# A row sum behind ReLU: the first load cut from 16 rows of each partition to one

## The chip, the core and the metric

The kernel runs on one core of a Trainium2 chip. The metric is the device time of one execution in microseconds (us). Three runs of the kernel before gave 161.19, 161.30 and 161.29 us; the median is 161.29.

The engines that matter here: ACT (ScalarE) and DVE (VectorE) compute, SP (SyncE) issues every DMA, and sixteen DMA engines move the data between HBM and the on-chip memory of 128 partitions.

## The reference

```python
def setup_inputs():
    batch, seq, dim = 32, 512, 1024
    return {"x": np.random.randn(batch, seq, dim).astype(np.float32)}

def reference(x):
    relu_x = np.maximum(x, 0)
    return np.sum(relu_x, axis=-1).astype(np.float32)
```

The input is 16,384 rows of 1,024 float32, 64 MiB; the output is one float32 for each row, 64 KiB.

## The kernel before, in words

**Tiling.** Each of the 128 partitions gets 128 rows. `x` is cut in two regions. The first holds 128 x 16 rows: partition p takes 16 rows that lie one behind the other, so the region is one stretch of 8 MB and the pitch from partition to partition is 64 KB. The second holds the other 14,336 rows, 112 for each partition, with a pitch of 448 KB. `rows(m, n)` and `sums(m, n)` (lines 85 and 90) choose the region for the rows m to m + n of each partition, for loads and stores.

**Stages.** Seven blocks of 16 rows (`ROWS`, 8,192 KB each) go through three buffers `io0` to `io2` of 64 KB for each partition. The eighth and last 16 rows are cut finer: a load of 8 rows, one of 4 (`TAIL = [8, 4]`), and then 4 rows as two loads of 1,164 and 642 KB and two small pieces (`piece0`, `piece1`, 120 and 122 KB). Row c + 2 of these four is put together from five parts: 280 elements of the first load, 260 of the second, the two pieces of 240 and 244, and a last reduction that also adds the other partial sums (line 224, 247 elements).

**Who computes.** In blocks 0 to 5 ACT clamps with ReLU in place (`clamp`, line 117) and DVE sums the clamped rows (`total`, line 125). `TWO` says in what steps: the whole block of 16 rows in blocks 0 to 2, twice 8 in blocks 3 and 4, twice 7 in block 5, where ACT does the two rows left by itself. A row alone is done in one instruction, either by ACT (`act_row`, line 132) or by DVE (`dve_row`, line 140). Block 6 is 9 rows of ACT and 7 of DVE. In the tail loads the rows alternate: row i goes to ACT if i is even, or if the load has 8 rows and i is 7, and otherwise to DVE.

**Order and waits.** The instructions of each engine run in the order of the program. `load` (line 99) issues on SP. The loads of blocks 0, 1 and 2 wait for nothing. The load of block j from 3 on waits until DVE is done with block j - 3 (`freed`), and the first tail load until DVE is done with block 4. Each load has a semaphore of its own, on which its first ACT row and, where DVE reads loaded rows, its first DVE row waits. A DVE sum waits for the ACT clamp before it. The stores stand behind all loads on SP: 16 sums of each partition (block 0), then 110, then the last 2 (`store`, line 110).

**Opening.** `open_without_barrier` puts the first `EARLY = 1` load ahead of everything else on SP and takes the opening barrier out.

Of the kernel before, what the change touches and what calls it, by code (L numbers as in the profile page):

```python
# [4 lines left out]
F32 = mybir.dt.float32  # L5
RELU = mybir.ActivationFunctionType.Relu
MAX, ADD = mybir.AluOpType.max, mybir.AluOpType.add
P = 128

ROWS = 16  # L10
# [3 lines left out]
TWO = [[16], [16], [16], [8, 8], [8, 8], [7, 7], []]  # L14
# [2 lines left out]

TAIL = [8, 4]  # L20
START_PIECE, END_PIECE = 280, 260
PIECES = [240, 244]

EARLY = 1


def kernel(tc: tile.TileContext, x: bass.AP, out: bass.AP):
    nc = tc.nc
    sems = Semaphores(tc)

    tc.close()
    tc.compile()
    nc.cur_bb = nc.bb_map[tc.start_bb_name]
    body = nc.cur_bb.bb.instructions
    ends = list(body)
    body.clear()
    n_stores = relu_sum(nc, sems, x, out)
    body.extend(ends)


    nc.cur_bb = nc.bb_map[tc.start_bb_name + "_end"]
    nc.cur_bb.bb.instructions.clear()
    nums = sorted(s.num for s in (*sems.loads, sems.act, sems.dve))
    cleared = range(nums[0], nums[-1] + 1)
    assert len(cleared) == len(nums)
    nc.sync.sem_clear(cleared)
    nc.sync.wait_ge(sems.stored, 16 * n_stores).then_inc(sems.stored, -16 * n_stores)
    open_without_barrier(tc, EARLY)


class Semaphores:
    def __init__(self, tc: tile.TileContext):
        n = len(TWO) + len(TAIL) + 2 + len(PIECES)
        self.loads = [tc.alloc_semaphore(f"load{i}") for i in range(n)]
        self.act = tc.alloc_semaphore("act")
        self.dve = tc.alloc_semaphore("dve")
        self.stored = tc.alloc_semaphore("stored")


def relu_sum(nc, sems: Semaphores, x: bass.AP, out: bass.AP):  # L60
    x_flat = x.flatten_outer_dims()
    N, D = x_flat.shape
    NT = N // P
    NB = len(TWO)
    assert N == P * NT == P * ROWS * (NB + 1)
    assert sum(TAIL) == ROWS - 4 and START_PIECE + END_PIECE + sum(PIECES) == D

    bufs = [nc.alloc_sbuf_tensor(f"io{i}", [P, ROWS, D], F32) for i in range(NBUF)]
    res = nc.alloc_sbuf_tensor("res", [P, NT], F32)

    extra = len(PIECES) + 1
# [3 lines left out]
    ]  # L75


    N1 = P * ROWS
    xf = x_flat[:N1].rearrange("(p m) d -> p m d", p=P)
    xv = x_flat[N1:].rearrange("(p m) d -> p m d", p=P)  # L80
    o_flat = out.rearrange("b s -> (b s)")
    of = o_flat[:N1].rearrange("(p m) -> p m", p=P)
    ov = o_flat[N1:].rearrange("(p m) -> p m", p=P)

    def rows(m, n):
        if m < ROWS:
            return xf[:, m : m + n, :]
        return xv[:, m - ROWS : m - ROWS + n, :]

    def sums(m, n):  # L90
        if m < ROWS:
            return of[:, m : m + n], res[:, m : m + n]
        return ov[:, m - ROWS : m - ROWS + n], res[:, m : m + n]

    n_load = n_act = n_dve = n_store = 0

    def load(dst, src, after=None):
        nonlocal n_load
        dma = nc.sync.dma_start(out=dst, in_=src)  # L99
        if after:  # L100
            dma.wait_op(sems.dve, after[1], "sem-ge")
        dma.then_inc(sems.loads[n_load], 16)
        n_load += 1
        return sems.loads[n_load - 1]

    def store(m, n, act, dve):
        nonlocal n_store
        dst, src = sums(m, n)
        nc.sync.wait_ge(sems.act, act)
        nc.sync.dma_start(out=dst, in_=src).wait_op(sems.dve, dve, "sem-ge").then_inc(  # L110
            sems.stored, 16
        )
        n_store += 1
# [24 lines left out]
    def dve_row(ap, accum_out, loaded):  # L138
        nonlocal n_dve
        i = nc.vector.tensor_scalar(  # L140
            out=ap,
            in0=ap,
            scalar1=0.0,
            scalar2=None,
            op0=MAX,
            op1=ADD,
            accum_out=accum_out,
        )
        if loaded is not None:
            i.wait_op(loaded, 16, "sem-ge")  # L150
        i.then_inc(sems.dve, 1)
        n_dve += 1

    freed = []
    m = 0
    for j in range(NB):
        buf = bufs[j % NBUF]
        loaded = load(buf[:, :, :], rows(m, ROWS), j >= NBUF and freed[j - NBUF])
        c = 0
        act_waits = dve_waits = loaded  # L160
        for n in TWO[j]:
            clamp(buf[:, c : c + n, :], act_waits)
            total(buf[:, c : c + n, :], m + c, n)
            act_waits = None
            c += n
        for _ in range(ACT[j]):
            act_row(buf[:, c, :], res[:, m + c : m + c + 1], act_waits)
            act_waits = None
            c += 1
        for _ in range(DVE[j]):  # L170
            dve_row(buf[:, c, :], res[:, m + c : m + c + 1], dve_waits)
            dve_waits = None
            c += 1
        assert c == ROWS
        freed.append((n_act, n_dve))
        m += ROWS
# [3 lines left out]
    c = 0  # L180
    for n in TAIL:
        loaded = load(
            buf[:, c : c + n, :], rows(m, n), None if c else freed[NB - NBUF]
        )
        for i in range(n):
            if i % 2 == 0 or (n == 8 and i == 7):
                act_row(buf[:, c, :], res[:, m : m + 1], loaded if i == 0 else None)
            else:
                dve_row(buf[:, c, :], res[:, m : m + 1], loaded if i == 1 else None)
            c += 1  # L190
            m += 1

    flat = buf[:, :, :].rearrange("p c d -> p (c d)")
    src = rows(m, 4).rearrange("p c d -> p (c d)")
    at = c * D
    split = 2 * D
# [4 lines left out]
    loaded = load(flat[:, at : at + b], src[:, :b])  # L201
    act_row(buf[:, c, :], res[:, m : m + 1], loaded)
    sums_act = n_act
    dve_row(buf[:, c + 1, :], res[:, m + 1 : m + 2], loaded)
    sums_dve = n_dve
    dve_row(flat[:, at + split : at + b], others[0], None)
    loaded = load(flat[:, at + end : at + 4 * D], src[:, end:])
# [7 lines left out]

    store(0, ROWS, *freed[0])
    store(ROWS, NT - ROWS - 2, sums_act, sums_dve)

    for i in range(len(PIECES) - 1):
        dve_row(parts[i][:, :], others[2 + i], arrived[i])
# [9 lines left out]
    ).wait_op(sems.dve, n_dve, "sem-ge").then_inc(sems.dve, 1)  # L232
    n_dve += 1
    store(NT - 2, 2, n_act, n_dve)
    return n_store


def open_without_barrier(tc: tile.TileContext, n_loads: int):

    SP = mybir.EngineType.SP
    blocks = tc.nc.main_func.blocks
    opening = blocks[0].instructions
    body = next(b for b in blocks if b.name == tc.start_bb_name).instructions
    for i in list(opening):
        if isinstance(i, (mybir.InstDrain, mybir.InstEventSemaphore)):
            opening.remove(i)
    loads = [i for i in body if i.engine == SP][:n_loads]
    for i in loads:  # L250
        assert isinstance(i, mybir.InstDMACopy)
        body.remove(i)
    at = next(n for n, i in enumerate(opening) if i.engine == SP)
    opening[at:at] = loads
# [30 lines left out]
```

## Time and profile before

One execution was profiled. Its span, from the first instruction to the last, is 159.6 us.

| | |
|---|---|
| median of three runs | 161.29 us |
| span of the profiled execution | 159.6 us |
| DVE busy | 117.6 us (74%) |
| ACT busy | 104.2 us (65%) |
| bytes moved | 67.18 MB, 421 GB/s over the span |
| DVE, sum of 16 rows | 17.22 us |
| DVE, sum of 8 rows | 8.68 us |
| ACT, clamp of 16 rows | 13.86 us |
| ACT, clamp of 8 rows | 7.02 us |
| ACT, one row with its sum | 1.05 us |
| DVE, one row with its sum | 1.21 us, a new one each 1.14 us |
| first load, issue to landing | 21.6 us |
| other blocks, issue to landing (median) | 26.9 us |

The shares of busy time are means over the whole span; the engines wait for different things in different parts of it, so single stretches have to be looked at. A DVE row is followed by a short read of the accumulator, and the next row starts while that is read. An arrow in square brackets behind a line of the timeline gives the engine's idle time before the instruction and what ended it.

### The profile page before, as it was taken

The page shows a single profiled execution, that of the slowest core. Times are in us where ns is not written, and L with a number is a line of the kernel's source. Part 1 is how long each engine was busy: PE and PEld are TensorE (multiplying, and loading weights), DVE is VectorE, ACT ScalarE, POOL GpSimd, SP SyncE. Part 2 cuts the span into 40 slices and gives each one's busy share as a digit, 9 for nine tenths or more (in the row PEclk, how much of TensorE's full clock was granted, in tenths as well). Part 3 has the DMA queues.
Part 4 walks back from the last instruction along what each step waited for, and adds up shares of the span by engine and source line. Part 5 has one row for each costly group of instructions (what it writes and reads, how often), then busy time and mean ns, then how long its engine had stood idle before and what let it go on. Part 6 is the DMA issues. An engine that isn't in the chain of part 4 may idle for free.

```text
span 159.6 us, 120 instructions
## 1 busy us (share of the span) xinstructions
DVE 117.6 (74%) x43; ACT 104.2 (65%) x50; POOL 0.2 (0%) x4
## 2 busy tenths in 40 slices
DVE  0000000009999499994999999999999999999986
ACT  3000059990699708996099951999329993499995
POOL 0000000000000000000000000000000000000000
DMA  7996996996997999979979969969969969798993
GB/s 279 509 526 263 526 526 263 526 509 279 526 476 312 526 394 394 526 345 443 526 328 460 526 263 526 526 263 526 509 279 526 493 296 526 337 452 382 418 412 119
DMA packets 2304, 67.18 MB, mean 421 GB/s; under 512 B 640, under 2 KB 896, under 8 KB 1024
## 3 DMA queue, kind: packets, MB, share of 16 engines
q1 hardware_dynamic: 2304, 67.18, 98.0%
HBM read 67.11 MB, written 0.07 MB: 421 GB/s over the span
## 4 chain that ended last, share of the span: by engine, by line
DMA 43%; DVE 34%; ACT 17%; another core or an unknown queue 3%; SPq 1%; issue 0%
DMA io<-in_x_dram 43%; DVE res L125 32%; ACT io L117 17%; DVE io L140 1%; SPq L99 1%; DVE piece L224 0%; DVE piece L140 0%
## 5 line engine op out<-in xcount | busy, mean ns | idle before, releaser
L125 DVE TENSOR_REDUCE res<-io 128x8 f32<-128x8192 f32 (+2 forms) x9 | 101.1, 11287 | 40.0 <-ACT io L117 40.0
L117 ACT ACTIVATE io<-io 128x8192 f32<-128x8192 f32 (+2 forms) x9 | 81.7, 9110 | 47.7 <-DMA io<-in_x_dram 47.7
L132 ACT ACTIVATE io<-io 128x1024 f32<-128x1024 f32 x20 | 20.9, 1045 | 6.0 <-DMA io<-in_x_dram 6.0
L140 DVE TENSOR_SCALAR_CACHE_REDUCE io<-io 128x1024 f32<-128x1024 f32 (+2 forms) x15 | 15.8, 1110 | 0.5 <-DMA io<-in_x_dram 0.4
L132 ACT ACTIVATION_READ_ACCUMULATOR io<-io 128x1 f32 x20 | 3.8, 188 | 0.0
L117 ACT ACT_TABLE_LOAD x1 | 1.3, 1283 | 0.1
L140 DVE DVE_READ_ACCUMULATOR io<-io 128x1 f32 x15 | 1.2, 82 | 0.0
L224 DVE TENSOR_SCALAR_CACHE_REDUCE piece<-piece 128x247 f32<-128x247 f32 x1 | 0.4, 410 | 0.0
L140 DVE TENSOR_SCALAR_CACHE_REDUCE piece<-piece 128x240 f32<-128x240 f32 x1 | 0.4, 397 | 0.0
L269 POOL MEMSET const-bfloat16-1.0<- 128x1 bf16 x1 | 0.1, 101 | 0.0
L269 POOL MEMSET const-uint8-127<- 128x1 uint8 x1 | 0.1, 101 | 0.0
L269 POOL MEMSET const-float32-0.0<- 128x1 f32 x1 | 0.1, 98 | 0.2 <-issue 0.2
L269 POOL MEMSET const-float32-1.0<- 128x1 f32 x1 | 0.1, 98 | 0.0
L224 DVE DVE_READ_ACCUMULATOR piece<-piece 128x1 f32 x1 | 0.1, 83 | 0.0
L140 DVE DVE_READ_ACCUMULATOR piece<-piece 128x1 f32 x1 | 0.1, 82 | 0.0
## 6 DMA issues: line engine op xcount, KB each, us to landing
io<-in_x_dram SPq DMA_DIRECT2D x1, 4096.0 KB, 21.6
io<-in_x_dram SPq DMA_DIRECT2D x1, 2048.0 KB, 26.1
io<-in_x_dram SPq DMA_DIRECT2D x1, 1164.0 KB, 28.4
io<-in_x_dram SPq DMA_DIRECT2D x1, 642.0 KB, 29.5
piece<-in_x_dram SPq DMA_DIRECT2D x1, 122.0 KB, 29.2
piece<-in_x_dram SPq DMA_DIRECT2D x1, 120.0 KB, 29.4
io<-in_x_dram SPq DMA_DIRECT2D x7, 26.9
out_dram<-res SPq DMA_DIRECT2D x1, 55.0 KB, 1.6
```

What stands on the lines that cost most here:

```text
L99: dma = nc.sync.dma_start(out=dst, in_=src)
L117: i = nc.scalar.activation(out=ap, in_=ap, func=RELU)
L125: nc.vector.tensor_reduce(out=res[:, m : m + n], in_=ap, axis=mybir.AxisListType.X, op=ADD).wait_op(sems.act, n_act, "sem-ge").then_inc(se ...
L132: i = nc.scalar.activation(out=ap, in_=ap, func=RELU, accum_out=accum_out)
L140: i = nc.vector.tensor_scalar(out=ap, in0=ap, scalar1=0.0, scalar2=None, op0=MAX, op1=ADD, accum_out=accum_out,)
L224: nc.vector.tensor_scalar(out=last[:, :], in0=last[:, :], scalar1=0.0, scalar2=None, op0=MAX, op1=ADD, accum_out=res[:, NT - 2 : NT - 1],) ...
L269: nc = _bacc.Bacc("TRN2", target_bir_lowering=False, num_devices=1)
```

## The change

The first region shrinks from 16 rows of each partition to one (`FIRST = 1`): 128 rows, 512 KB, one stretch, loaded into a buffer of its own (`ahead`, 4 KB for each partition). It is now the load that stands ahead of everything. DVE does this row with `dve_row`, ahead of its other work. The seven blocks follow as before, from the second region, which now has 127 rows for each partition and a pitch of 508 KB. As one row has been done by then, the first tail load has 7 rows in place of 8. The first store carries one sum for each partition, and doesn't wait for ACT; the second carries 125.

```diff
-TAIL = [8, 4]
+TAIL = [7, 4]
+FIRST = 1
...
+    ahead = nc.alloc_sbuf_tensor("ahead", [P, FIRST, D], F32)
...
-    N1 = P * ROWS
+    N1 = P * FIRST
     xf = x_flat[:N1].rearrange("(p m) d -> p m d", p=P)
     xv = x_flat[N1:].rearrange("(p m) d -> p m d", p=P)
...
     def rows(m, n):
-        if m < ROWS:
+        if m < FIRST:
             return xf[:, m : m + n, :]
-        return xv[:, m - ROWS : m - ROWS + n, :]
+        return xv[:, m - FIRST : m - FIRST + n, :]
...
-        nc.sync.wait_ge(sems.act, act)
+        if act:
+            nc.sync.wait_ge(sems.act, act)
...
+    loaded = load(ahead[:, :, :], rows(0, FIRST))
+    for m in range(FIRST):
+        dve_row(ahead[:, m, :], res[:, m : m + 1], loaded if m == 0 else None)
+    sums_ahead = n_act, n_dve
     freed = []
-    m = 0
+    m = FIRST
     for j in range(NB):
...
-    store(0, ROWS, *freed[0])
-    store(ROWS, NT - ROWS - 2, sums_act, sums_dve)
+    store(0, FIRST, *sums_ahead)
+    store(FIRST, NT - FIRST - 2, sums_act, sums_dve)
```

More of the change, by code (lines that the diff above doesn't have):

```diff
@@ L52, in __init__ @@
     def __init__(self, tc: tile.TileContext):
-        n = len(TWO) + len(TAIL) + 2 + len(PIECES)
+        n = 1 + len(TWO) + len(TAIL) + 2 + len(PIECES)
         self.loads = [tc.alloc_semaphore(f"load{i}") for i in range(n)]
@@ L65, in relu_sum @@
     assert N == P * NT == P * ROWS * (NB + 1)
-    assert sum(TAIL) == ROWS - 4 and START_PIECE + END_PIECE + sum(PIECES) == D
+    assert sum(TAIL) == ROWS - FIRST - 4 and START_PIECE + END_PIECE + sum(PIECES) == D
     bufs = [nc.alloc_sbuf_tensor(f"io{i}", [P, ROWS, D], F32) for i in range(NBUF)]
+    ahead = nc.alloc_sbuf_tensor("ahead", [P, FIRST, D], F32)
     res = nc.alloc_sbuf_tensor("res", [P, NT], F32)
@@ L85, in rows @@
     def rows(m, n):
-        if m < ROWS:
+        if m < FIRST:
             return xf[:, m : m + n, :]
-        return xv[:, m - ROWS : m - ROWS + n, :]
+        return xv[:, m - FIRST : m - FIRST + n, :]
     def sums(m, n):
-        if m < ROWS:
+        if m < FIRST:
             return of[:, m : m + n], res[:, m : m + n]
-        return ov[:, m - ROWS : m - ROWS + n], res[:, m : m + n]
+        return ov[:, m - FIRST : m - FIRST + n], res[:, m : m + n]
     n_load = n_act = n_dve = n_store = 0
```

## The prediction

> **What bounds the kernel now.** I read the page's DMA part first, then the busy time by stages cut at the arrivals of the blocks, then the chain that ended last, then the timeline of the end. Page and stages:
>
> ```profile
> q1 hardware_dynamic: 2304, 67.18, 98.0%
> ```
>
> ```profile
> 0.00:21.87 21.87, 0.00 (x0) 1.28 (x2) 0.20 (x4) 1.00 1.02 432
> 21.87:41.19 19.32, 5.43 (x1) 13.86 (x2) 0.00 (x0) 1.00 1.00 434
> 79.90:99.25 19.35, 19.35 (x2) 13.95 (x2) 0.00 (x0) 1.00 1.00 434
> ```
>
> The sixteen DMA engines are occupied 98% of the span, and a block of 8,192 KB takes 19.35 us in the middle of the stream (columns: stretch, its length, busy DVE, ACT, POOL, clock, DMA share, GB/s). So a row of each partition (512 KB) is 19.35 / 16 = 1.21 us. The third line also shows DVE busy for all of its 19.35 us: there are two full resources, not one. The chain says where each of them leads:
>
> ```profile
> 60.55 13.87 ACT io L117
> 74.41 0.02 issue
> 74.44 51.60 DVE res L125 x5
> ...
> 126.91 28.43 DMA io<-in_x_dram
> 155.34 0.02 issue
> 155.37 2.02 DVE io L140 x6
> 157.39 0.33 DVE piece L140 x2
> ```
>
> ACT takes block 2 the moment it lands (60.53), DVE starts on it at 74.44, and from there DVE does not stop: the timeline's next idle mark on DVE, beyond gaps of a few hundredths, is the one below. At the end the last loads and DVE arrive nearly together, which these lines of the timeline of DVE show (start, length, then the idle time before it):
>
> ```profile
> 151.26 1.21 DVE L140 TENSOR_SCALAR_CACHE_REDUCE io<-io 128x1024 f32<-128x1024 f32 x1
> 152.40 0.08 DVE L140 DVE_READ_ACCUMULATOR io<-io 128x1 f32 x1
> 152.56 1.22 DVE L140 TENSOR_SCALAR_CACHE_REDUCE io<-io 128x1024 f32<-128x1024 f32 x1
> ...
> 154.85 0.08 DVE L140 DVE_READ_ACCUMULATOR io<-io 128x1 f32 x1
> 155.37 1.22 DVE L140 TENSOR_SCALAR_CACHE_REDUCE io<-io 128x1024 f32<-128x1024 f32 x1 [0.43 <-DMA io<-in_x_dram]
> ...
> 156.88 0.08 DVE L140 DVE_READ_ACCUMULATOR io<-io 128x1 f32 x1
> 156.95 0.42 DVE L140 TENSOR_SCALAR_CACHE_REDUCE io<-io 128x260 f32<-128x260 f32 x1
> ```
>
> In an unbroken run a row starts where the accumulator read of the row before starts. Against that pace DVE stands still 152.56 - 152.40 = 0.16 us for the four-row load, 155.37 - 154.85 = 0.52 us for the 1,164 KB load, and 156.95 - 156.88 = 0.07 us for the 642 KB load. The first two, 0.68 us, are the whole reserve of DVE against the stream; the third is a last 0.07.
>
> **The change, part by part.**
>
> 1. *The first load becomes 512 KB, every block arrives later.* In the stream 512 KB more go ahead of block 0: 1.21 us. It is one more load with 128 more descriptors. What a load costs beyond its bytes is read from the small ones at the end, by their arrivals (the starts above, and ACT's, which waits for the 642 KB load and starts at 156.95): 1,164 KB from 152.56 to 155.37 is 2.81 us, where 1,164 / 8,192 x 19.35 = 2.75; 642 KB from 155.37 to 156.95 is 1.58, where 1.52 is due. So 0.06 us. Bounds are 0.00 (block behind block: 19.35 with no gap that grows) and 0.08. I take 0.07, and blocks 0 to 6 land 1.28 us later.
>
> 2. *The last loads do not arrive later by that.* The tail load has seven rows in place of eight, so the 1.21 us is given back there; the four-row load, the 1,164 KB, the 642 KB and the two pieces land 0.07 us later than now. The total of bytes is what it was.
>
> 3. *The issues on SP.* SP issues the first three loads at the start in 1.33 us (the timeline has them as one group from 0.00), about 0.43 us apart; now it is four loads, none with a wait. Load two is issued 0.43 us behind the first, whose transfer takes 1.21 us, so the queue has work: cover 0.78 us. If the cover is gone, both the blocks and the last loads move (rival A). The later loads wait on SP for DVE to free a buffer. The first of these: DVE ends block 0 at 35.76 + 17.22 = 52.98, while the stream has work until 60.53; both move by 1.28, so 7.5 us of cover remains, and for the next one it is (55.08 + 17.22 = 72.30 against 79.88) the same. Behind such a waiting load stand all later loads and the three stores, which as now are not due before 129. The first store loses its wait for ACT and carries 4 bytes for each partition in place of 64; it is queued behind the pieces and done long before the last store, which waits for DVE's last row. Three stores as before: 0.
>
> 4. *One DVE row at the front.* One row of 1.21 us on `ahead`, with its wait for the first load. Behind it in DVE's queue is the reduction of block 0, which started at 35.76 after idling from the start. The row is done by some 6 us, so 30 us of cover: 0. If the cover were gone it would cost 1.21 once.
>
> 5. *One ACT row fewer in the tail.* With eight rows ACT took 0, 2, 4, 6 and 7; with seven it takes 0, 2, 4, 6. DVE keeps 1, 3, 5. So ACT's list loses 1.04 us while its start on block 6 moves by 1.28: ACT is 0.24 us later where it idles 0.30 us before the 1,164 KB load and 0.44 before the 642 KB load (timeline of ACT). Covered: 0.07, with the load. **DVE's list from block 0 to the end is as long as before.** The row that was taken from the tail was ACT's.
>
> 6. *DVE's lateness.* Its unbroken run starts with block 2's arrival, so it moves from 74.44 to 75.72 and all behind it by 1.28. Of this, the two gaps give back 0.68, as the loads that DVE waits for there have moved by no more than 0.07 and are there when it comes: the row that started at 155.37 can start at 154.85 - 0.16 + 1.28 = 155.97, against an arrival of 155.41. Late by 0.60; the 0.07 before the 260-element piece is used up too: 0.53. The rest (260, 240 and 247 elements) runs without a wait for a load, since the last pieces land before 157.74 + 0.07. The last store waits for DVE's last result, so the end moves by the same.
>
> Sum: +1.28 - 0.68 - 0.07 = **+0.53 us**. Span 159.6 + 0.53 = 160.1. The median of the runs, 161.29, is 1.7 us above the span; this lies around the span and nothing in the change touches it. Time 161.29 + 0.53 = **161.82**. From bounds of part 1 (0.00 to 0.08), and 0.1 for the spread of the runs (161.19 to 161.30): 161.65 to 162.0.
>
> 7. *The pitch.* Rows for it: block 0 has a pitch of 64 KB, blocks 1 to 6 of 448 KB, and the stages give 432 and 434 GB/s, the first with the start-up in it. Pitch has made no difference between those; 508 KB is not in the trace. The nearest row is 448 KB: 0. Upper bound: below.
>
> The Trainium skill, page DMA: Bandwidth & Descriptors, section Latency and other measured facts, has a row on HBM row pitch: 512 KiB ran at 207 GB/s and 4 MiB with 4 KiB added at 214, the full rate there. No run here shows 512 KiB; 508 KiB lies 4 KiB off it, so the rule would leave the rate alone, and by its 512 KiB figure, 3% lower, the sum would be some 4.7 us more.
>
> The same page's Rules for kernel authors ask for at least 1 MiB per DMA, and its section on the anatomy of one DMA gives a fixed cost of about 2.0 us, for the other queue kind; this speaks against a first load of 512 KB. The trace disagrees for a load with others behind it in the queue (0.06 us over its bytes); by the rule the sum would be about 2.5 us.
>
> **Rivals.**
>
> A. *The queue runs dry behind the small load.* For it: block 0 lands 21.87 us after the start where a block in the stream takes 19.35, so a first load has 2.5 us of start-up, and if the second load's start-up isn't hidden behind 1.21 us of transfer, a hole opens. Against: the issues are 0.43 apart, so the second should be ready 0.78 us early. A hole shifts all arrivals and DVE alike. Bounds: 0 to 1.4 us (the smallest store's whole way from issue to landing); half way 0.7 gives 161.82 + 0.7 = 162.5.
>
> B. *The 508 KB pitch is slower.* 0.4% on some 155 us of stream is 0.6 us, from where loads, not DVE, set the end; at 1% it is 161.29 + 1.55 + 0.07 = 162.9, at 3% 166.0. Against: two pitches seven times apart run alike.
>
> C. *The start-up shrinks* (the other side). Of the 2.5 us, part may belong to sixteen engines opening 64 KB stretches over 8 MB; now they open 4 KB rows within 512 KB. A saving s moves the blocks and the last loads alike: 161.82 - s. It can't exceed 2.5 - 1.4 = 1.1 (160.7). From s = 0.21 it is no change, from 0.85 faster. At the middle, 0.55: 161.27. For it: no row of a 4 KB opening. Against: 0.38 of the 2.5 is the issue, and the rest is mostly the way of the first and last bytes, which a small load has too.
>
> **How the numbers follow.** Forecast 0.62, A 0.12, B 0.06, C 0.20 (0.08 of it faster). About 0.2%, 0.32 us, is what a measurement of this kernel tells from no change: below 160.97 faster, above 161.61 slower. Slower: 0.60 + 0.12 + 0.06 = 0.78; same: 0.02 of the forecast and 0.12 of C, 0.14; faster 0.08. The range: down into C to 161.35, up through A to 162.7, leaves out B, the lower half of C and the top of A, some 0.2. The forecast's own is 161.65 to 162.0.
>
> **What would show it.** Right: ACT starts on block 0 at about 23.15, on block 2 at 61.83; DVE's unbroken run begins at 75.7; no idle mark on DVE for a DMA behind it; ACT still idles before its last two rows; the last piece lands where it did. Wrong: block 0 after 23.4 (A) or before 22.9 (C); blocks more than 19.4 apart (B); DVE idle for the 1,164 KB load. The forecast falls if DVE's reserve, 0.68 us read from one execution, is larger in the others, or if rows on DVE don't hold 1.14 us.

## The result, and the profile after

| | before | after |
|---|---|---|
| median, same chip | 161.24 us (4 runs, 161.16 to 161.30) | 165.78 us (4 runs, 165.56 to 166.92) |
| ratio | | 1.0305, 95% interval 1.0282 to 1.0327 |
| span of the profiled execution | 159.6 us | 164.4 us |
| last reduction of DVE starts | 157.74 us | 158.01 us |
| from that start to the end of the span | 1.9 us | 6.4 us |

The kernel became 3% slower. The last row of the table says where: DVE ends 0.27 us later than before, but the program ends 4.8 us later. The loss lies behind the last instruction that computes.

The end of the chain of waits, after (start, length, what):

```profile
75.49 66.64 DVE res L129 x7
142.13 15.34 DVE io L144 x29
...
157.66 0.33 DVE piece L144 x2
158.01 0.42 DVE piece L232 x2
```

DVE's unbroken run now reaches from 75.49 to the end. No DMA line stands between, where there was one before (126.91 to 155.34): DVE is the last to come, as forecast.

Stages of the profile after, cut at ACT's starts on blocks 0, 1, 2 and 3 (stretch, length, busy DVE, ACT and POOL, clock, DMA share, GB/s):

```profile
22.86:42.21 19.35, 5.46 (x1) 13.86 (x1) 0.00 (x0) 1.00 1.00 434
42.21:61.60 19.39, 17.26 (x2) 13.86 (x1) 0.00 (x0) 1.00 1.00 433
61.60:80.93 19.33, 17.16 (x2) 13.86 (x2) 0.00 (x0) 1.00 1.00 434
```

At a pitch of 508 KB the blocks come 19.33 to 19.39 us apart, at 433 to 434 GB/s. The loads are as fast as at 448 KB.

The stores in the list of DMA issues (what, engine, operation, count, KB, us from issue to landing), before:

```profile
out_dram<-res SPq DMA_DIRECT2D x1, 55.0 KB, 1.6
out_dram<-res SPq DMA_DIRECT2D x1, 8.0 KB, 28.8
out_dram<-res SPq DMA_DIRECT2D x1, 1.0 KB, 1.4
```

and after:

```profile
out_dram<-res SPq DMA_DIRECT2D x1, 62.5 KB, 5.8
out_dram<-res SPq DMA_DIRECT2D x1, 0.5 KB, 29.9
out_dram<-res SPq DMA_DIRECT2D x1, 1.0 KB, 5.9
```

All three stores count up one semaphore, 16 steps each, and a store's landing is read as the time at which that count is full for it (16, 32, 48). So a late step of the first store looks like a late landing of the next ones; what SP waits for at the end is the whole count.

The last store, 1 KB as ever, takes 5.9 us where it took 1.4: 4.5 us more. With DVE's 0.27 this is 4.77 of the 4.8. SP's own waits show the same at the end, where it waits for all stores to have landed; before:

```profile
SPq L47 <- SPq L47: 1.0, 1, 1.0
```

and after:

```profile
SPq L49 <- SPq L49: 5.5, 1, 5.5
```

The page after cuts the span into 40 slices of 4.1 us; what the DMA engines move in the last three is 411, 58 and 0 GB/s. So in the last slice the trace counts no data, and only steps of the semaphore still come in: at the end it is the reports of landing that are late.

Nothing in the bytes explains it (62.5 KB and 1 KB). Two things in the stores are new: the first one writes 128 times 4 bytes into one stretch of 512 bytes, and the others have a pitch of 508 bytes, which isn't a multiple of 64, where they had 448.

### The profile page after: what moved, and what is told of

Its sections match the earlier page's. It is cut to its first block, busy times and chain, and to the rows that moved or that the text cites. A ratio compares the mean times of both kernels' runs of the same rounds, so it can differ in the third digit from the quotient of the medians.

```text
span 164.4 us, 120 instructions
## 1 busy us (share of the span) xinstructions
DVE 118.6 (72%) x45; ACT 103.1 (63%) x48; POOL 0.2 (0%) x4
## 2 busy tenths in 40 slices
DMA packets 2448, 67.18 MB, mean 409 GB/s; under 512 B 656, under 2 KB 912, under 8 KB 1168
## 3 DMA queue, kind: packets, MB, share of 16 engines
q1 hardware_dynamic: 2448, 67.18, 95.1%
## 4 chain that ended last, share of the span: by engine, by line
DVE 50%; DMA 25%; ACT 17%; another core or an unknown queue 3%; SPq 0%; issue 0%
DVE res L129 41%; DMA io<-in_x_dram 25%; ACT io L121 17%; DVE io L144 9%; SPq L102 0%; DVE piece L232 0%; DVE piece L144 0%
## 5 line engine op out<-in xcount | busy, mean ns | idle before, releaser
L136 ACT ACTIVATE io<-io 128x1024 f32<-128x1024 f32 x19 | 19.8, 1045 | 6.0 <-DMA io<-in_x_dram 6.0
L144 DVE TENSOR_SCALAR_CACHE_REDUCE ahead<-ahead 128x1024 f32<-128x1024 f32 x1 | 1.2, 1220 | 3.4 <-DMA ahead<-in_x_dram 3.4
```

The source lines that it names most:

```text
L136: i = nc.scalar.activation(out=ap, in_=ap, func=RELU, accum_out=accum_out)
L144: i = nc.vector.tensor_scalar(out=ap, in0=ap, scalar1=0.0, scalar2=None, op0=MAX, op1=ADD, accum_out=accum_out,)
```

## The experiments

The runs of the kernel before on the chips of the experiments had medians of 161.04 to 161.06 us.

### Stores or loads: two that cross them

**All stores at a pitch of 512 bytes.** Loads and compute as in the change.

```diff
-        if m < FIRST:
-            return of[:, m : m + n], res[:, m : m + n]
-        return ov[:, m - FIRST : m - FIRST + n], res[:, m : m + n]
+        grid = o_flat.rearrange("(p m) -> p m", p=P)
+        return grid[:, m : m + n], res[:, m : m + n]
```

> Loads and compute of the changed kernel; only the addresses of the three stores move, to a pitch of 512 bytes (the sums land in another order in the output). The 4.5 us of the result are the time from the issue of a store to its landing (5.8 and 5.9 us now, 1.4 and 1.6 before). Theory S (128 writes of 4 bytes into the same 512 bytes hold up every later completion): 161.5 us, the last two stores land in 1.4 to 1.7 us. Theory P (a pitch of 508 bytes in the second and third store, so that neighbours write into the same lines): also 161.5. Rival L (the loads' pitch of 508 KB does it): 165.8, landing stays at 5.8. Rival F (a 4-byte write is slow by itself, wherever it goes): 165 or more.

Measured: 161.31 us, ratio to before 1.0017 (1.0007 to 1.0026). Its DMA issues:

```profile
out_dram<-res SPq DMA_DIRECT2D x1, 62.5 KB, 1.5
out_dram<-res SPq DMA_DIRECT2D x1, 0.5 KB, 27.7
out_dram<-res SPq DMA_DIRECT2D x1, 1.0 KB, 1.4
```

The same stores of the same sizes: the last two land in 1.5 and 1.4 us. The loads' pitch (L) and the bare size of 4 bytes (F) fall.

**The loads of before with the stores of the change.**

```diff
-    store(0, ROWS, *freed[0])
-    store(ROWS, NT - ROWS - 2, sums_act, sums_dve)
+    store(0, 1, *freed[0])
+    store(1, NT - 1 - 2, sums_act, sums_dve)
```

with the first into `o_flat[:P]` and the others, 127 to a partition, behind it.

> The kernel before, with its loads, its row order and its compute, but stores cut and placed as in the change: 1, 125 and 2 sums for each partition, the first into one stretch of 512 bytes, the others at a pitch of 508 bytes (the sums land in another order). Theories S and P: 161.3 + 4.2 = 165.5, landings of 5 to 6 us. Rival L: 161.3, landings of 1.4 to 1.6.

Measured: 165.47 us, ratio 1.0285 (1.0260 to 1.0309). Its DMA issues:

```profile
out_dram<-res SPq DMA_DIRECT2D x1, 62.5 KB, 5.7
out_dram<-res SPq DMA_DIRECT2D x1, 0.5 KB, 30.5
out_dram<-res SPq DMA_DIRECT2D x1, 1.0 KB, 5.6
```

The old loads with the new stores lose 4.4 us. The cause is in the stores alone.

### Which store

**Without the first store.**

```diff
-    store(0, FIRST, *sums_ahead)
```

> The changed kernel without its first store, the one of 4 bytes for each partition, so 128 sums are not written. Theory S: 161.5 us, last stores land in 1.4 to 1.7 us. Theory P: 165.8, landing about 5.8. If both take part: between, with landings between 1.6 and 5.8.

Measured: 161.33 us, ratio 1.0018 (1.0009 to 1.0028). Its DMA issues:

```profile
out_dram<-res SPq DMA_DIRECT2D x1, 62.5 KB, 1.6
out_dram<-res SPq DMA_DIRECT2D x1, 1.0 KB, 1.4
```

The two other stores, at their pitch of 508 bytes, are fast. Theory P falls: it is the store of 512 bytes, and it costs 4.54 - 0.27 = 4.3 us (each time against the kernel before on its own chip: 165.78 - 161.24 and 161.33 - 161.06).

**The first store early**, behind the load of block 2:

```diff
+        if j == NBUF - 1:
+            store(0, FIRST, *sums_ahead)
...
-    store(0, FIRST, *sums_ahead)
```

> The changed kernel with its first store issued behind the load of block 2, so that its writes are done some 100 us ahead of the end; nothing is left out. Theory S: 161.5 us, the last two stores land in 1.4 to 1.7 us. Theory P: 165.8. Both: between, as much below 165.8 as the kernel without this store.

Measured: 166.76 us, ratio 1.0359 (1.0344 to 1.0375): a miss for every theory, and the most telling run. Its stores at the end land in 1.6 and 1.4 us, as theory S has it. But the time is lost elsewhere. ACT's timeline (start, length, instruction, idle before it and what ended it):

```profile
42.27 13.86 ACT L121 ACTIVATE io<-io 128x16384 f32<-128x16384 f32 x1 [5.49 <-DMA io<-in_x_dram]
61.65 13.86 ACT L121 ACTIVATE io<-io 128x16384 f32<-128x16384 f32 x1 [5.53 <-DMA io<-in_x_dram]
86.74 13.95 ACT L121 ACTIVATE io<-io 128x8192 f32<-128x8192 f32 x2 [11.23 <-DMA io<-in_x_dram]
106.10 7.03 ACT L121 ACTIVATE io<-io 128x8192 f32<-128x8192 f32 x1 [5.41 <-DMA io<-in_x_dram]
```

From block 2 to block 3, between which the store is queued, it is 25.09 us, where the stretches on either side have 19.38 and 19.36. The stages say it from the DMA's side (61.58 to 80.91, then the next block's length):

```profile
61.58:80.91 19.33, 17.17 (x2) 13.86 (x1) 0.00 (x0) 1.00 0.75 271
80.91:100.25 19.34, 18.30 (x2) 13.51 (x2) 0.00 (x0) 1.00 1.00 434
```

In that stretch 271 GB/s are moved instead of 434. So more than the report is late: here the store keeps the DMA engines from the load behind it, for 25.09 - 19.35 = 5.7 us. In the middle of a full stream nothing hides this. At the end of the kernel 4.3 of it show; that DVE's last rows hide the rest fits the times, but was not tried by itself. The sixteen reports of this store in the trace spread from 61.64 to 67.73 us, so its parts finish far apart.

### How closely packed

The first store's 4-byte writes at other pitches, the other stores beside them in their own region; for a pitch of 64 bytes (G = 16):

```diff
+        G = 16
+        if m < FIRST:
+            few = o_flat[: P * G].rearrange("(p m) -> p m", p=P)
+            return few[:, m : m + n], res[:, m : m + n]
+        many = o_flat[P * G :].rearrange("(p m) -> p m", p=P)
```

> The changed kernel, its first store writing 4 bytes for each partition at a pitch of 64 bytes (the others at 448; 15 sums of each partition are not written). The first store held the queue 5.7 to 6.1 us with all 128 writes in 512 bytes, and not visibly at a pitch of 512. If what holds it is several writes into the same 64 bytes: 161.3 us, landings 1.4 to 1.6 us. If it is the same 512 bytes (8 writes in each now, 128 before), in turn: a sixteenth of 5.8 us, 0.4, on the landings, 161.6. If all writes that lie close are done one after the other: 165.5.

> As the run with a pitch of 64 bytes, at a pitch of 16 (the others at 496; 3 sums of each partition are not written). Same 64 bytes, in turn: 4 writes in each in place of 16, a quarter of 5.8 us: 1.4 us more on the landings, some 162 to 162.7. Same 512 bytes, in turn: 32 in each in place of 128, the same quarter. Told apart by the run at 64: none left there (64 bytes) or 0.4 us (512 bytes). All one after the other: 165.5.

> The changed kernel, its first store at a pitch of 8 bytes (the others at 504; one sum of each partition is not written). At a pitch of 4 the store took 5.7 to 6.1 us, at 16 nothing in the time (161.34). At 16 the four neighbouring partitions fill 64 bytes, at 8 eight share 64 bytes, at 4 sixteen. Theory X (what costs is that writes of several DMA engines meet in the same 64 bytes): clearly slow, 162.5 to 164. Theory N (only the number of writes in a stretch matters, smoothly): between the run at 16 and the changed kernel too, but nearer to the run at 16, 161.4 to 162. If it stays at 161.3, it takes the full packing.

| pitch of the 4-byte writes | time, us | ratio (95% interval) | second store, issue to landing | last store |
|---|---|---|---|---|
| 4 bytes (the change) | 165.78 | 1.0305 (1.0282 to 1.0327) | 5.8 | 5.9 |
| 8 bytes | 162.91 | 1.0114 (1.0100 to 1.0127) | 2.9 | 2.8 |
| 16 bytes | 161.34 | 1.0018 (1.0009 to 1.0027) | 2.2 | 1.4 |
| 64 bytes | 161.29 | 1.0015 (1.0006 to 1.0024) | 1.6 | 1.4 |
| 512 bytes | 161.31 | 1.0017 (1.0007 to 1.0026) | 1.5 | 1.4 |

In all five rows of the table the trace counts 2,448 DMA packets, so the packed store isn't cut into more pieces than the others; only where the pieces go differs.

The run at 16 was expected at 162 to 162.7 and missed; the landing of its second store tells why. The count for that store is still full late (2.2 for 1.6), but the one for the last store isn't: the hold is over before DVE's last result is there. If the hold of 5.7 us halves with each doubling of the pitch, it is 2.9 at 8 and 1.4 at 16. The last store then lands 5.9 - 2.8 = 3.1 us earlier at 8 than at 4, where 2.9 is due, and at 16 the hold fits between the landing of the last piece and the last store. This agrees with a hold that grows with the number of writes in a stretch; only the one at a pitch of 4 was measured directly.

**Groups that meet.** The run at 8 bytes had come out where theory X put it (162.5 to 164), so X was tried for itself: the pitch of 16 and the count stay, the start moves by 32 bytes.

```diff
+        OFF, G, H = 8, 4, 120
+        if m < FIRST:
+            few = o_flat[OFF : OFF + P * G].rearrange("(p m) -> p m", p=P)
+            return few[:, m : m + n], res[:, m : m + n]
+        many = o_flat[P * 8 : P * (8 + H)].rearrange("(p m) -> p m", p=P)
```

> The changed kernel, first store of 4 bytes at a pitch of 16 bytes, starting 32 bytes behind a multiple of 64; the other stores at a pitch of 480 (7 sums of each partition are not written). In each 64 bytes there are 4 writes as without the offset, but two of one group of four neighbouring partitions and two of the next. Theory X (groups that meet in the same 64 bytes): clearly slower than without the offset, 162 to 163 us. Theory C (the count of writes in 64 bytes): as without the offset, 161.3.

> As the run with the offset, but the first store starts at a multiple of 64, so that each 64 bytes belong to one group of four neighbouring partitions. Both theories: 161.3 us, as the earlier run at a pitch of 16.

Measured: 161.26 (ratio 1.0014, 1.0005 to 1.0024) with the offset, 161.28 (1.0012, 1.0002 to 1.0021) without. The second store lands in 2.4 and 2.5 us. No difference: theory X falls as tried here, at a pitch at which the time shows no hold anyway. Of the theories tried, the density of the writes is what is left. Over what stretch the writes are counted, 64 bytes, 512 or another, these runs don't tell.

### The 0.27 us of DVE

**Without the first store, and DVE on block 2 6.9 us earlier.**

```diff
-TWO = [[16], [16], [16], [8, 8], [8, 8], [7, 7], []]
+TWO = [[16], [16], [8, 8], [8, 8], [8, 8], [7, 7], []]
```

> The changed kernel without its first store (128 sums are not written), and block 2 done in two steps of 8 rows in place of 16, so that DVE starts on it 6.9 us earlier. Without this step the same kernel ran 161.33 us, 0.27 above the kernel before on that chip, with DVE's last reduction at 158.02. Theory: that rest is DVE's lateness alone. Then DVE idles again before the 1,164 KB load, its last reduction starts at about 157.6, and the time is 160.9, 0.15 below the kernel before. Rival: the rest belongs to the stores or the loads; then it stays at 161.3.

Measured: 160.99 us, ratio 0.9997 (0.9988 to 1.0005), against 161.33 without this step. DVE's timeline:

```profile
155.32 1.22 DVE L144 TENSOR_SCALAR_CACHE_REDUCE io<-io 128x1024 f32<-128x1024 f32 x1 [0.42 <-DMA io<-in_x_dram]
...
157.71 0.41 DVE L231 TENSOR_SCALAR_CACHE_REDUCE piece<-piece 128x247 f32<-128x247 f32 x1
```

DVE idles again before the 1,164 KB load, and its last reduction starts at 157.71, not 158.02. The rest was DVE's lateness. What remains isn't told from the kernel before.

**The kernel before with the same step** (`TWO` alone):

> The kernel before with block 2 in two steps of 8 rows, nothing else. DVE idled before the 1,164 KB load there, so it isn't what ends the kernel: no change, 161.06 us, ratio 1.000. A gain of 0.1% or more would say that the step itself, not the small first load, made the gain of the run without the first store and with DVE early.

Measured: 161.07 us, ratio 1.0002 (0.9994 to 1.0011). No change, as expected: there DVE was not what came last.

### Other layouts, and a version that mends the store

**One region at a pitch of 512 KB.**

```diff
-        if m < FIRST:
-            return xf[:, m : m + n, :]
-        return xv[:, m - FIRST : m - FIRST + n, :]
+        return x_flat.rearrange("(p m) d -> p m d", p=P)[:, m : m + n, :]
```

with stores of 126 and 2 sums at 512 bytes, and `TWO` as above.

> One region of 128 rows for each partition: all loads at a pitch of 512 KB, all stores at 512 bytes (126 and 2 sums; no store of 4 bytes), one row first, block 2 in two steps. Nothing left out. It tells whether the loads' pitch matters at all near 508 KB. If loads don't care about the pitch: blocks 19.35 us apart as at 448 and 508 KB, 160.9 to 161.0 us. If a pitch of 512 KB is slow, as the Trainium skill's figures of 207 against 214 GB/s for copies within HBM suggest (DMA: Bandwidth & Descriptors, Latency and other measured facts; 3%): blocks some 20.0 apart, 165.7 us.

Measured: 161.38 us, ratio 1.0016 (1.0007 to 1.0025). ACT's timeline, one line for each arrival of blocks 0 to 4:

```profile
23.14 13.86 ACT L118 ACTIVATE io<-io 128x16384 f32<-128x16384 f32 x1 [21.73 <-DMA io<-in_x_dram]
42.48 13.86 ACT L118 ACTIVATE io<-io 128x16384 f32<-128x16384 f32 x1 [5.48 <-DMA io<-in_x_dram]
61.98 13.95 ACT L118 ACTIVATE io<-io 128x8192 f32<-128x8192 f32 x2 [5.65 <-DMA io<-in_x_dram]
81.72 13.95 ACT L118 ACTIVATE io<-io 128x8192 f32<-128x8192 f32 x2 [5.79 <-DMA io<-in_x_dram]
101.04 13.95 ACT L118 ACTIVATE io<-io 128x8192 f32<-128x8192 f32 x2 [5.37 <-DMA io<-in_x_dram]
```

Distances of 19.34, 19.50, 19.74 and 19.32 us: two blocks lose 0.15 and 0.4, the others nothing. The 3% were not there, and neither was the gain. Why two blocks were late stays open; single distances of 19.51 and 19.49 us stand in ACT's timelines of the run at 8 bytes (61.75 to 81.26) and of the run below with the sums turned (42.35 to 61.84) too, with loads at 508 KB, so only the 0.4 was seen at 512 KB alone.

**One row out of the 16-row region**, the other 15 as the tail, blocks at 448 KB:

```diff
+        if m < FIRST + MID:
+            return xv[:, m - FIRST : m - FIRST + n, :]
+        return xf[:, m - MID : m - MID + n, :]
```

> Nothing left out. The first load takes one row of each partition out of a region of 16 rows (4 KB rows at a pitch of 64 KB), the tail loads take the other 15 of that region, the blocks lie in the 112-row region (pitch 448 KB) as before; so no store writes less than 8 bytes in a place or into a neighbour's 64 bytes. Block 2 in two steps. Theory: landings 1.4 to 1.6 us, DVE not late, 160.9 us, against 161.06 to 161.29 before: faster by about 0.1%. If the shorter start-up of the small load (block 0 at 22.84 where 23.15 was due) needs its 512 KB in one stretch, block 0 lands at 23.15 and the time is 161.2, no gain.

Measured: 161.48 us, ratio 1.0023 (1.0013 to 1.0032). ACT starts on block 0 at 23.16, where it was 22.86 with the contiguous 512 KB: the second branch of the expectation. The contiguous openings of the other runs landed block 0 between 22.82 and 23.02, this one at 23.14 and the run at 512 KB at 23.11; so 0.1 to 0.3 us of the start-up seem to depend on how the first load lies. The time is worse than the 161.2 of that branch. The row behind the 1,164 KB load starts at 155.82 against 155.32 in the run with DVE early, so 0.5 us are lost, most of it in the loads behind the opening. The landings in the two traces say where: against the run with DVE early, block 0 lands 0.15 us later, block 6 0.24 (139.34 and 139.10) and the seven-row load 0.54 (148.15 and 147.61). That load is the first that goes back to the 16-row region; why it takes 0.3 us longer stays open.

**The sums turned.** The change with its first store as 4 writes of 128 bytes, after a 32 by 32 turn on DVE, and `TWO` as above.

```diff
+        nc.vector.transpose(out=turned[:, :], in_=wide[:, :]).wait_op(
+            sems.dve, n_dve, "sem-ge"
+        ).then_inc(sems.dve, 1)
...
-    store(0, FIRST, *sums_ahead)
+    nc.sync.dma_start(
+        out=o_flat[:P].rearrange("(a b) -> a b", a=4), in_=turned[::32, :]
+    ).wait_op(sems.dve, sums_ahead[1], "sem-ge").then_inc(sems.stored, 16)
```

> The changed kernel, nothing left out, with the first store mended: DVE turns the 128 sums of the first load (32 by 32 blocks) so that they lie in 4 partitions of 32, at 5 us where it idles, and the store writes 4 times 128 bytes; block 2 in two steps. If the packed 4-byte writes were all of the loss: landings 1.4 to 1.7 us and the time of the run without this store and with DVE early, 160.99; level with the kernel before (161.06) or faster by up to 0.1%. If writes below 512 bytes that share a stretch are slow whatever their size: landings above 2 us, over 161.5.

Measured: 161.10 us, ratio 1.0005 (0.9990 to 1.0019). DVE's timeline at the start:

```profile
4.52 0.08 DVE L165 DVE_READ_ACCUMULATOR ahead<-ahead 128x1 f32 x1
4.64 0.21 DVE L175 STREAM_TRANSPOSE turned<-wide 128x32 f32<-128x32 f32 x1
```

The turn takes 0.21 us in DVE's idle time, and SP's last wait is back at 1.0 us. The same 512 bytes in the same place cost nothing as four writes of 128 bytes. The time is level with the kernel before, 3% below the change. None of these versions beats the kernel before by more than the measurement tells.

## Why the prediction was wrong, point by point

**The step that failed** is part 3, in the words "Three stores as before: 0" and, of the first store, "done long before the last store". The change cuts that store from 64 bytes to 4 for each partition, and with it packs all 128 writes into 512 bytes. I counted stores and bytes, and looked at what the store waits for, not at where it writes. Such a store held up the stream for 5.7 us where it stood in the middle of it; where the change has it, it costs 4.3 us of the time. It is not done before the last store either: without it, the last two stores land in 1.6 and 1.4 us, with it in 5.8 and 5.9. I had priced the new pitch of the loads and given a rival to it, but the same line of the diff moves the output's addresses too, and no step of the sum spoke of those.

**The first load (part 1)** was 0.29 us too dear. Block 0 was due at 23.15 and ACT starts on it at 22.86: +1.0 and not +1.28. This is rival C at a small size; the two layouts that open with rows far apart came later (23.14 and 23.16), which speaks for the contiguous opening, though single profiles of one layout differ by 0.2 too. The last loads (part 2), due 0.07 us later than before, came earlier by about as much as that saving leaves: ACT starts on the last two at 155.16 and 156.77, where it was 155.36 and 156.95. (The first load before took 21.8 us from issue to landing; the 21.6 us in the table of the profile before are the eight-row tail load's.)

**DVE's lateness (part 6)** was the right mechanism with the wrong size. Without the packed store the time is 161.33 and 161.31, +0.25 to +0.27 over the kernel before, where +0.53 was due. The missing 0.26 agrees with the start-up: DVE's run starts at 75.49 (75.72 due), it never idles for a load until the end, and ACT still idles before its last two rows (0.48 and 0.46 us), all as named. That it is this lateness was shown by taking it away (160.99).

**Pitch of the loads (part 7, rival B):** as taken, 0. The 3% that the Trainium skill's figure for 512 KiB (DMA: Bandwidth & Descriptors, Latency and other measured facts) would have given didn't come even at 512 KB; that figure was measured on copies between HBM tensors, and these are loads to the on-chip memory.

**Rival A** fell: no hole behind the small load. The 2.0 us fixed cost for a DMA (same page, the anatomy of one DMA), told there for another queue kind, did not show in this position.

**The direction** was forecast as slower, for a cost that is real but a sixteenth of the one that decided (0.27 and 4.3 us). That cost alone, 161.33 against 161.06, stays under the 0.32 us that the prediction calls told from no change. That the kernel became clearly slower, as forecast, was luck.

## What to carry to other kernels

When a change moves how rows are dealt to partitions, read the store side of the diff as closely as the load side: for every store, how many bytes each partition writes and at what pitch. A store of one 4-byte word for each of 128 partitions into one packed row was cheap in bytes and dear in time here; turn it on an idle engine first, or let each partition write 64 bytes or more, as the kernel before does. A slow store is not harmless because it is issued early: here it stopped the load behind it in the queue.

## What the runs showed of the hardware

- 128 writes of 4 bytes packed into 512 bytes held the DMA queue 5.7 us. If they were taken one after another, which no run shows, that would be some 45 ns for each, as an estimate (5.7 / 128). At a pitch of 8 bytes the kernel lost 1.85 us (162.91 against 161.06, DVE's 0.27 in it). At pitches of 64 and 512 bytes the same writes cost nothing that the time shows.
- The Trainium skill (DMA: Bandwidth & Descriptors, Specifications) says that transfers under 512 bytes become a read-modify-write. Whether that is behind the hold, no run here shows; the size alone isn't enough, since 4 bytes at a pitch of 64 or 512 ran in 161.29 and 161.31 us.
- The hold reaches the work behind the store: in the middle of the stream it cut a stretch of 19.33 us from 434 to 271 GB/s. At the end of the kernel, where no load is left, only the reports come late. What inside the DMA engines waits, no run here tells.
- Stores with a pitch of 508 bytes, whose neighbours share 64 bytes at their edges, landed in 1.6 us, as at 448.
